# Three adaLN vectors summed on GpSimd beside the attention, a fourth on VectorE in the first FFN, and P scaled on VectorE

## The chip, the cores and the metric

One core of one Trainium2 chip runs the kernel; nothing is shared with other cores. The time is that of one execution on the device, in microseconds (us); lower is better. A profile is taken of one execution of its own.

## The reference, cut to what matters

Two layers of a diffusion transformer over 512 latent tokens of 1024 channels, with 256 context tokens. The first layer mixes tokens by attention (4 heads of global attention, 4 of windowed attention), the second by a Fourier transform; each layer ends in a gated FFN with a width-3 convolution. Six vectors for each layer (shift, scale and gate of both sub-layers) come from a matrix-vector product with the conditioning vector; four of the first layer's six are what the change is about.

```python
def adaln_params(cond, w, bias):
    m = jax.nn.silu(cond) @ w + bias                     # (1024) @ (1024, 6 * 1024)
    return jnp.split(m[..., None, :], N_MOD, axis=-1)
...
def attend(q, k, v, sink=None):
    s = jnp.einsum('bqkgd,bskd->bkgqs', q, k, preferred_element_type=F32) * (HEAD_DIM ** -0.5)
    ...
        p = jax.nn.softmax(s, axis=-1)
    return jnp.einsum('bkgqs,bskd->bqkgd', p.astype(v.dtype), v)
...
    for i in range(DEPTH):
        sh1, sc1, g1, sh2, sc2, g2 = adaln_params(c, mod_w[i], mod_b[i])
        h = modulate(rms_norm(x, norm_g[i, 0]), sh1, sc1)
        ...
        x = x + g1 * rms_norm(y, norm_g[i, 1])
        h = modulate(rms_norm(x, norm_g[i, 2]), sh2, sc2)
        x = x + g2 * rms_norm(conv_ffn(h, ...), norm_g[i, 3])
```

## The kernel before

All of it is fp32. A product is made of three (`mm3`, L90 to L92): both operands are split into a high part (a ScalarE copy to fp32r) and a low part (the difference, on VectorE or now and then GpSimd; `split`, L113). Activations lie with channels on partitions: `xT`, `yT`, `hh` and `hl` are 128 x 8 x 512.

The stages, in order: the start (shift and scale, keys and values of two heads, up to about 100 us); the other projections; the attention with the rest of the query projections beside its first heads (about 120 to 275 us); the output projection and the first FFN; the Fourier mixer; the second FFN.

*The attention.* Eight heads, one after the other, each with four blocks of 128 queries (32 blocks). For a block TensorE makes the scores (`S`), VectorE their maximum (L854) and the exponent's bias (L857 in heads 0 to 3, L862 in heads 4 to 7), ScalarE the exponential into `P` with its sum (L864). In heads 4 to 7, which have a sink, L867 and L868 add the sink's term to the sum. L869 takes the reciprocal, and L870 multiplies the 128 x 768 (or 640, or 512) block of P by it, on GpSimd. TensorE transposes P (`PT`, L786), ScalarE and VectorE split it, and TensorE multiplies it with the values (`O`). The products with the values run one head behind the scores.

*Work beside the attention.* `rest` is a Python generator that issues the query projections of heads 2 to 7 (`gm`, with their rotary part in `roped`, L637 to L643, partly on GpSimd); `gem0` issues the adaLN products. After each half block the kernel advances one of them by the number of steps in its table `FILL`: `rest` in heads 0 to 3, `gem0` in heads 4 to 7.

*The adaLN vectors.* A matrix-vector product of 1024 x 1024 for each. Vectors 0 and 1 of layer 0 are made in the start. `gemv_pe` makes 2 to 5: for two vectors at a time it loads eight 1 MB tiles, 128 rows of the matrix each, and TensorE multiplies each with one column of the conditioning vector, in four column groups (L405); then a copy (L409), four transposes (L412), and one addition of the bias. `gemv_jobs` makes the six of layer 1 in the first FFN: eight multiply-adds of 128 x 1024 on VectorE (L376, L379), the sum over partitions by TensorE (L384), two transposes. There, `pump(gem, ...)` advances it by one step for each of 19 hidden tiles (11 in the first half, 8 in the second) and by two for each of 8 output tiles, 35 steps in all; a vector takes five steps.

*What sets the order.* The kernel is traced in the order of the Python code, and a planner with a model of each engine's times orders the instructions on each engine; an engine then executes its list in order and waits where a semaphore isn't yet there. Work traced late may be put early if its inputs are there. Loads go through SyncE's queue, in order. All weights pass through three 1 MB buffers (`raw`, L121).

*Who needs the vectors.* Vector 2 (as `der[:, 0, 1]`) is the gate after the output projection, 3 and 4 make the input of the first FFN, right after it. Vector 5 (as `der[:, 0, 3]`) is the gate after the first FFN, some 400 us later.

Of the kernel before, what the change touches and what calls it, by code (L numbers as in the profile page):

```python
# [34 lines left out]
# what is traced where: how far work of one kind runs ahead of another kind's  # L35
# [6 lines left out]
# products that keep the PE's clock up: at the start, before the first sums' use, before the second FFN  # L42
# [25 lines left out]
def kernel(ctx: ExitStack, tc: tile.TileContext, a):  # L68
# [25 lines left out]
    # issued after another one on the same engine  # L94
# [4 lines left out]
    # work that must not be issued ahead of the last instruction traced before a fence on its engine  # L99
# [61 lines left out]
    # products that keep the PE's clock up where it would have to wait  # L161
# [4 lines left out]
    # sums over channels: four column tiles of the PE hold a quarter of the tokens each  # L166
# [5 lines left out]
    # 1 / sqrt(sum / D + eps)  # L172
# [10 lines left out]
    # the same where only the time until the end counts: sums on all partitions at once  # L183
# [14 lines left out]
    # one quarter of the tokens per quadrant of partitions: side by side, then to all partitions  # L198
# [12 lines left out]
    # h = x * am * R + bm for several channel tiles, shared out over the engines  # L211
# [15 lines left out]
    # squares of y: summed over channel tiles by GpSimd, the last one by the PE  # L227
    class YStat:
# [8 lines left out]
        def add(self, pps, src, hs):  # L237
# [9 lines left out]
            # the halves of the last one share a tile where they come one after the other  # L247
# [26 lines left out]
    # x += gate * rms_norm(y) for one channel tile  # L274
# [11 lines left out]
    # x += gate * rms_norm(y); then the next sub-layer's modulated input  # L286
# [56 lines left out]
        # the factors: tokens on partitions, or on all partitions  # L343
# [23 lines left out]
    # adaLN off the critical path: products and sums on DVE, the sum over partitions on the PE  # L367
    def gemv_jobs(jobs, pps):
        for l, v in jobs:
            acc = mk(cp, [P, D], F32, "gacc", 1)  # L370
            for kk in range(4):
                w = raw([P, 2, D], a["mod_r"][v, kk])
# [9 lines left out]
            ps = mk(pps, [P, T], F32, "misc", 2)  # L382
            for j in range(4):
                PE.matmul(ps[32 * j:32 * j + 32, :256], lhsT=ones32, rhs=acc[:, j * 256:(j + 1) * 256], start=True,  # L384
                          stop=True)
            rs = mk(cp, [P, T], F32, "sq", 2)
            S.copy(out=rs[:, :256], in_=ps[:, :256])
            tp = mk(pps, [P, T], F32, "misc", 2)
            for b in range(2):
                PE.transpose(out=tp[:, b * P:(b + 1) * P], in_=rs[:, b * P:(b + 1) * P], identity=ident)  # L390
# [4 lines left out]
            derive(l, v)  # L395
# [1040 lines left out]
```

## Time and profile before

| | |
|---|---|
| median of 3 runs | 1181.5 us (1178.45 to 1182.66) |
| span of the profiled execution, first to last instruction | 1176.5 us |
| the profiled execution's own time | given as its span alone |
| instructions | 17,135 |
| mean granted TensorE clock | 0.988 of full speed |
| TensorE (PE) busy | 1134.0 us, 96% |
| VectorE (DVE) busy | 751.6 us, 64% |
| ScalarE (ACT) busy | 512.2 us, 44% |
| GpSimd (POOL) busy | 201.1 us, 17% |
| moved by DMA | 145.18 MB |

A row of a group reads: line, engine, operation, tile written <- tiles read, shapes, number of instructions | busy us in all, mean ns of one | idle time of the engine just before them, and what ended it. A row of the timeline reads: start, duration (both us), engine, line, operation, tiles, shapes; "x2" joins two instructions that follow each other, with the time from the first's start to the last's end. A row of a stretch has the busy time of each engine in it, then the granted clock, the DMA engines' busy share and GB/s. TensorE's busy time is modelled; a matmul's record overlaps with the next one's, so path shares tell more of it than sums of durations. The busy time of an instruction on VectorE or GpSimd includes what it waits after it has been issued.

### The profile page before, as it was taken

How to read it: one execution, taken by the hardware profiler on the slowest of the kernel's cores; microseconds unless marked ns; L12 is line 12 of the kernel's file. 1: busy time of each engine (PE TensorE's matmuls, PEld its weight loads, DVE VectorE, ACT ScalarE, POOL GpSimd, SP SyncE). 2: the span in 40 equal slices, each digit the busy share in tenths (PEclk: the TensorE clock that was granted, in tenths of full speed). 3: DMA queues.
4: the chain of work that ended last, by engine and by line, in shares of the span. 5: the costliest groups of instructions: out<-in, count | busy, mean ns of one | idle time of the engine just before them, and what ended most of it. 6: DMA issues, size and time to landing. Idle time of an engine off the chain costs nothing.

```text
span 1176.5 us, 17135 instructions
## 1 busy us (share of the span) xinstructions
PE 1134.0 (96%) x6878; PEld 946.1 (80%) x6878; DVE 751.6 (64%) x1215; ACT 512.2 (44%) x887; POOL 201.1 (17%) x213
## 2 busy tenths in 40 slices
PE   7999999999999999999999998988999999999995
PEld 4689898679898877777878998877788888888895
DVE  4673777675779685756665568988966532255555
ACT  3332356566554434322444445646644332234342
POOL 1132534222320000000000153663000000000013
PEclk9999999999999999999999999998999999999998
DMA  9432110874115353666622301621233222332112
GB/s 371 187 127 72 37 36 7 298 306 152 65 43 209 108 208 110 237 238 225 233 90 56 116 11 35 210 81 60 72 108 103 73 84 99 108 108 72 54 55 72
DMA packets 27127, 145.18 MB, mean 123 GB/s; under 512 B 2724, under 2 KB 7460, under 8 KB 14120
## 3 DMA queue, kind: packets, MB, share of 16 engines
q1 hardware_dynamic: 27048, 144.09, 35.0%
q8 instruction: 54, 0.88, 0.3%
q14 instruction: 25, 0.20, 0.1%
HBM read 141.98 MB, written 2.10 MB: 122 GB/s over the span
## 4 chain that ended last, share of the span: by engine, by line
PE 84%; DVE 11%; DMA 1%; ACT 1%; issue 1%; POOL 1%; SPq 0%; DVEq 0%; ACTq 0%; POOLq 0%
PE mm L90 24%; PE mm L92 23%; PE mm L91 23%; DVE md_t L278 2%; PE PT L786 2%; PE gm L405 1%; DVE hl L333 1%; PE O L90 1%; DVE wl L113 1%; DVE xT L280 1%; PE S L90 1%; PE O L91 1%; PE O L92 1%; PE S L92 1%; DMA xT<-in_xT 1%
## 5 line engine op out<-in xcount | busy, mean ns | idle before, releaser
L113 DVE TENSOR_TENSOR wl<-raw,wh 128x1024 fp32r<-128x1024 f32 (+1 forms) x139 | 167.6, 1210 | 207.8 <-ACT wh L113 207.5
L90 PE MATMUL mm<-hh,wh 128*128 128x512 f32 (+2 forms) x728 | 276.1, 379 | 0.0
L92 PE MATMUL mm<-hh,wl 128*128 128x512 f32 (+2 forms) x728 | 275.7, 379 | 0.0
L91 PE MATMUL mm<-hl,wh 128*128 128x512 f32 (+2 forms) x728 | 275.4, 378 | 0.0
L113 ACT CAST wh<-raw 128x1024 fp32r<-128x1024 f32 (+2 forms) x151 | 149.6, 999 | 183.4 <-PE mm L91 141.9
L90 PEld LDWEIGHTS mm<-hh,wh 128*128 128x128 f32 x728 | 137.7, 189 | 29.3 <-issue 1.2
L92 PEld LDWEIGHTS mm<-hh,wl 128*128 128x128 f32 x728 | 137.7, 189 | 27.9
L91 PEld LDWEIGHTS mm<-hl,wh 128*128 128x128 f32 x728 | 137.8, 189 | 27.5
L253 POOL TENSOR_TENSOR gacc<-gacc,sq 128x256 f32<-128x256 f32 (+1 forms) x35 | 31.5, 900 | 681.3 <-ACT sq L251 680.5
L90 PE MATMUL mm<-xh,wh 128*128 128x512 f32 (+1 forms) x368 | 131.5, 357 | 0.0
L91 PE MATMUL mm<-xl,wh 128*128 128x512 f32 (+1 forms) x368 | 130.6, 355 | 0.0
L92 PE MATMUL mm<-xh,wl 128*128 128x512 f32 (+1 forms) x368 | 130.5, 355 | 0.0
L90 PEld LDWEIGHTS mm<-xh,wh 128*128 128x128 f32 x368 | 69.2, 188 | 12.4 <-issue 1.2
L91 PEld LDWEIGHTS mm<-xl,wh 128*128 128x128 f32 x368 | 69.1, 188 | 11.1
L92 PEld LDWEIGHTS mm<-xh,wl 128*128 128x128 f32 x368 | 69.0, 187 | 11.0
L113 ACT CAST xh<-cv 128x512 fp32r<-128x512 f32 x44 | 27.3, 620 | 100.9 <-DVE cv L1008 100.9
L995 DVE SCALAR_TENSOR_TENSOR cv<-mm,cols,cv 128x511 f32<-128x511 f32 x83 | 61.8, 745 | 11.4 <-ACT cv L994 11.4
L994 ACT ACTIVATE cv<-mm,cols 128x512 f32<-128x512 f32 x83 | 64.2, 774 | 10.4 <-PE mm L92 10.4
L997 DVE SCALAR_TENSOR_TENSOR cv<-mm,cols,cv 128x511 f32<-128x511 f32 x83 | 62.2, 749 | 2.2
L1007 ACT ACTIVATE cv<-cv 128x512 f32<-128x512 f32 x44 | 27.8, 631 | 71.2 <-DVE cv L997 68.7
L379 DVE SCALAR_TENSOR_TENSOR gacc<-raw,scol,gacc 128x1024 f32<-128x1024 f32 x42 | 53.8, 1281 | 4.5 <-DMA raw<-in_mod_r 4.1
L91 PE MATMUL mm<-hl,xh 128*128 128x256 f32 (+1 forms) x160 | 47.3, 296 | 3.6 <-DVE hl L333 2.8
(358 smaller groups left out, 2238.7 us busy)
## 6 DMA issues: line engine op xcount, KB each, us to landing
raw<-in_w_up SPq DMA_DIRECT2D x44, 1024.0 KB, 5.0
raw<-in_mod_r SPq DMA_DIRECT2D x24, 1024.0 KB, 5.0
raw<-in_mod_p SPq DMA_DIRECT2D x16, 1024.0 KB, 6.4
raw<-in_w_down SPq DMA_DIRECT2D x16, 896.0 KB, 4.6
raw<-in_w_down SPq DMA_DIRECT2D x16, 512.0 KB, 3.7
raw<-in_w_in SPq DMA_DIRECT2D x6, 1024.0 KB, 5.0
raw<-in_w_out SPq DMA_DIRECT2D x4, 1024.0 KB, 6.0
raw<-in_w_f SPq DMA_DIRECT2D x8, 512.0 KB, 4.4
```

Source lines behind the costliest of these rows:

```text
L90: i = PE.matmul(out, lhsT=ah, rhs=bh, start=start, stop=False)
L91: PE.matmul(out, lhsT=ah, rhs=bl, start=False, stop=False)
L92: return i, PE.matmul(out, lhsT=al, rhs=bh, start=False, stop=stop)
L113: i = S.copy(out=h, in_=src), eng.tensor_tensor(out=l, in0=src, in1=f(h), op=ALU.subtract)
L253: G.tensor_tensor(out=self.acc[:, sl], in0=self.acc[:, sl], in1=sq[:, sl], op=ALU.add)
L278: m = V.scalar_tensor_tensor(out=t, in0=yT[:, k, hs], scalar=der[:, l, gi, k:k + 1], in1=R, op0=ALU.mult, op1=ALU.mult)
L379: held(V.scalar_tensor_tensor(out=acc, in0=w[:, i, :], scalar=scol[:, 0, k:k + 1], in1=acc, op0=ALU.mult, op1=ALU.add))
L786: PE.transpose(out=pt[:, j * P:(j + 1) * P], in_=Ps[j][:, off:off + P], identity=ident)
L994: S.activation(out=cv, in_=ps, func=AF.Identity, bias=bc, scale=wc[1])
L995: V.scalar_tensor_tensor(out=cv[:, 1:], in0=ps[:, :T - 1], scalar=wc[0], in1=cv[:, 1:], op0=ALU.mult, op1=ALU.add)
L997: V.scalar_tensor_tensor(out=cv[:, :T - 1], in0=ps[:, 1:], scalar=wc[2], in1=cv[:, :T - 1], op0=ALU.mult, op1=ALU.add)
L1007: S.activation(out=cg, in_=cg, func=AF.Silu)
```

## The change

Four things are edited; everything else in the diff is comments that are taken out.

- `gemv_pe` goes. `gemv_pool` makes the vectors 2, 3 and 4 in halves of 512 columns: GpSimd multiplies each 128 x 512 piece of the matrix by the conditioning vector's column (in place in `raw`) and adds it to `pacc`, eight pieces for each half; four small products on TensorE sum over the partitions and bring the result to partitions at once; VectorE adds the bias. A step of the generator has two pieces.
- It is advanced by one step after each of the 32 query blocks, in all heads. Heads 4 to 7 have no entries in `FILL` any more. A vector takes nine steps, three take 27.
- Vector 5 becomes the first job of `gemv_jobs` in the first FFN, ahead of layer 1's six: seven jobs of five steps.
- L870 is issued on VectorE instead of GpSimd.

The matrix is laid out anew in memory: twelve tiles of 1 MB for `gemv_pool`, and four more for `gemv_jobs`, in place of sixteen for `gemv_pe`.

```diff
 FILL = [[1, 0, 1, 2, 3, 2, 1, 2],
...
-        [2, 1, 1, 0, 0, 1, 1, 2],
-        [2, 0, 0, 1, 1, 0, 2, 0],
-        [1, 0, 1, 0, 1, 0, 1, 0],
-        [2, 0, 1, 0, 0, 0, 1, 1],
-        [1, 0, 0, 0, 2, 1, 2, 0]]
+        [2, 1, 1, 0, 0, 1, 1, 2]]
...
     def gemv_jobs(jobs, pps):
...
-                w = raw([P, 2, D], a["mod_r"][v, kk])
+                w = raw([P, 2, D], a["mod_r"][6 * l + v - 5, kk])
...
-    def gemv_pe(pps):
-        for j in range(2):
-            ps = mk(pps, [P, T], F32, "gm", 1)
-            for k in range(KC):
-                w = raw([P, 2048], a["mod_p"][j, k])
-                for q in range(4):
-                    PE.matmul(ps[32 * q:32 * q + 32, :], lhsT=spad[:, k, :], rhs=w[:, q * T:(q + 1) * T],
-                              start=k == 0, stop=k == KC - 1)
-                yield
...
+    def gemv_pool(vs, pool, pps):
+        for v in vs:
+            for h in range(2):
+                acc = mk(pool, [P, T], F32, "pacc", 1)
+                for k in range(KC):
+                    if k % 4 == 0:
+                        w = raw([P, 4, T], a["mod_a"][v - 2, h, k // 4])
+                    sc = scol[:, 0, k:k + 1]
+                    t = w[:, k % 4, :] if k else acc
+                    G.tensor_scalar(out=t, in0=w[:, k % 4, :], scalar1=sc, scalar2=0.0, op0=ALU.mult, op1=ALU.add)
+                    if k:
+                        G.tensor_tensor(out=acc, in0=acc, in1=t, op=ALU.add)
+                    if k % 2:
+                        yield
+                ps = mk(pps, [P, T], F32, "PT", 2)
+                for b in range(4):
+                    PE.matmul(ps[:, 2 * b:2 * b + 2], lhsT=acc[:, b * P:(b + 1) * P], rhs=ones32[:, :2], start=True,
+                              stop=True)
+                mo = C_MB + v * KC + 4 * h
+                V.tensor_tensor(out=mods[:, 0, v, 4 * h:4 * h + 4],
+                                in0=ps[:, :8].rearrange("p (b r) -> p b r", r=2)[:, :, 0], in1=cols[:, mo:mo + 4],
+                                op=ALU.add)
+            derive(0, v)
             yield
...
-            gem0 = gemv_pe(aps)
+            gem0 = gemv_pool([2, 3, 4], at, aps)
...
-                    G.tensor_scalar(out=pr[:, :n], in0=pr[:, :n], scalar1=mx[:, 4:5], scalar2=0.0,
-                                    op0=ALU.mult, op1=ALU.add)
+                    V.tensor_scalar(out=pr[:, :n], in0=pr[:, :n], scalar1=mx[:, 4:5], scalar2=None, op0=ALU.mult)
...
                     for i in range(2):
                         pump(pend)
-                        pump(rest if is_a else gem0, FILL[head][2 * j + i])
+                        if is_a:
+                            pump(rest, FILL[head][2 * j + i])
+                    pump(gem0)
...
-                 gemv_jobs([(1, v) for v in range(6)], pps))
+                 gemv_jobs([(0, 5)] + [(1, v) for v in range(6)], pps))
...
-    mod_p = i['mod_w'][0].reshape(KC, P, 3, 2048)[:, :, 1:].transpose(2, 0, 1, 3)
+    mod_a = mw[0, :, :, 2:5].reshape(2, 4, P, 3, 2, T).transpose(3, 4, 0, 2, 1, 5)
```

More of the change, by code (lines that the diff above doesn't have):

```diff
@@ L365, in derive, with gemv_end @@
             V.tensor_tensor(out=der[:, l, n, :], in0=mods[:, l, v, :], in1=ng(l, n), op=ALU.mult)
+    def gemv_end(l, v, acc, pps, tag, bufs):
+        ps = mk(pps, [P, T], F32, tag, bufs)
+        for j in range(4):
+            PE.matmul(ps[32 * j:32 * j + 32, :256], lhsT=ones32, rhs=acc[:, j * 256:(j + 1) * 256], start=True,
+                      stop=True)
+        rs = mk(cp, [P, T], F32, "sq", 2)
+        S.copy(out=rs[:, :256], in_=ps[:, :256])
+        tp = mk(pps, [P, T], F32, tag, bufs)
+        for b in range(2):
+            PE.transpose(out=tp[:, b * P:(b + 1) * P], in_=rs[:, b * P:(b + 1) * P], identity=ident)
+        mo = C_MB + l * 48 + v * KC
+        V.tensor_tensor(out=mods[:, l, v, :].rearrange("p (j b) -> p j b", b=2),
+                        in0=tp[:, :256].rearrange("p (b j r) -> p j b r", b=2, r=32)[:, :, :, 0],
+                        in1=cols[:, mo:mo + KC].rearrange("p (j b) -> p j b", b=2), op=ALU.add)
+        derive(l, v)
     def gemv_jobs(jobs, pps):
@@ L381, in gemv_jobs @@
                 yield
[L382 to L390, printed above, removed]
@@ L1414, in _layout @@
     xT = chan(i["x"][0]).reshape(P, KC, 2, HT).transpose(0, 2, 1, 3)
[L1415 removed]
+    out.update(cols=cols, gqk=np.concatenate(rep[1:], 1), xT=xT, cT=chan(i["ctx"][0]), mod_s=mod_s, mod_r=mr[5:], mod_a=mod_a, w_kva=kva, w_in=np.stack(wi),
                w_out=w_out, w_up=w_up, w_f=w_f, w_ny=wf[:, P])
```

20 lines of the change are left out of this document (2 added, 18 removed).

## The prediction

> **What bounds the kernel now.** I read the summary first, then the chain of work that ended last, then the busy times of the stretches in which the change lies.
>
> ```profile
> span 1176.5 us, 17135 instructions
> PE 1134.0 (96%) x6878; PEld 946.1 (80%) x6878; DVE 751.6 (64%) x1215; ACT 512.2 (44%) x887; POOL 201.1 (17%) x213
> PE 84%; DVE 11%; DMA 1%; ACT 1%; issue 1%; POOL 1%; SPq 0%; DVEq 0%; ACTq 0%; POOLq 0%
> ...
> core 0: us, PE busy (x) PEld busy (x) DVE busy (x) ACT busy (x) POOL busy (x), PEclk, DMA share, GB/s
> 120.00:201.00 81.00, 77.70 (x550) 72.67 (x549) 61.01 (x124) 41.94 (x74) 32.17 (x31) 1.00 0.08 27
> 201.00:260.00 59.00, 59.00 (x426) 39.52 (x425) 42.01 (x102) 34.67 (x83) 13.25 (x17) 1.00 0.74 272
> 420.00:600.00 180.00, 180.00 (x799) 141.97 (x798) 117.99 (x131) 62.11 (x82) 0.00 (x0) 1.00 0.57 204
> ```
>
> TensorE carries 84% of the chain and GpSimd stands idle for 83% of the span, so the idea of moving sums from the one to the other looks sound at first sight. The two stretches of the attention differ. In the first, 120 to 201 us (heads 0 to 3), VectorE is busy for 61.0 of 81 us and GpSimd for 32.2. In the second, 201 to 260 us (heads 4 to 7), TensorE never pauses: the adaLN products that the change removes are mixed into it. The chain of that stretch shows how much they are.
>
> ```profile
> by line: PE gm L405 27.7%; PE PT L786 14.7%; PE O L90 11.2%; PE O L92 7.8%; PE O L91 7.7%; PE S L90 4.6%; PE S L846 4.0%; PE S L847 4.0%; PE S L848 3.9%; PE S L92 3.6%; PE S L91 3.2%; PE S L851 2.7%; PE PT L816 2.3%; PE gm L412 1.5%; PE S L
> ```
>
> **What TensorE loses and gets.** L405, the adaLN products, is 27.7% of 59 us = 16.3 us of the path, and L412, the transposes behind it, 1.5% = 0.9 us. Both go: -17.2 us, all of it in heads 4 to 7. Back come six groups of four products of a 128x128 block with two columns, one group for each half vector. The kernel has a line of that form in its Fourier part, and the first FFN has the form of the seventh job:
>
> ```profile
> 702.75 0.95 PE L349 MATMUL misc<-ones,yT 128*128 128x2 f32 x8
> 413.20 0.64 PE L384 MATMUL misc<-gacc,ones 128*32 128x256 f32 x8
> ```
>
> Four such products (eight records) take 0.95 us, so six groups take 5.7 us, half of it in heads 0 to 3. TensorE alone would gain 17.2 - 5.7 = 11.5 us. The seventh job adds 0.64 us and two transposes to the first FFN, where TensorE is full: +1 us. Its eight VectorE instructions are hidden there: VectorE is busy for 118 of 180 us between 420 and 600, and eight more at the durations of the rows below (one of 0.75, seven of 1.28 us) are 9.7 us; without that cover they would cost all of it.
>
> **What the P scaling costs VectorE.** L870 leaves GpSimd. The nearest VectorE row is L376, the same operation with a per-partition factor from SBUF to SBUF.
>
> ```profile
> L870 POOL TENSOR_SCALAR P<-P,mx 128x768 f32<-128x768 f32 x16 | 14.7, 916 | 39.1 <-DVE mx L869 31.8 <-PE PT L786 5.7 <-DVE qrs L150 1.5
> L870 POOL TENSOR_SCALAR P<-P,mx 128x640 f32<-128x640 f32 x8 | 7.3, 907 | 27.5 <-ACT th L113 7.0 <-DVE mx L869 6.4 <-DVE mx L862 5.3
> L870 POOL TENSOR_SCALAR P<-P,mx 128x512 f32<-128x512 f32 x8 | 5.6, 697 | 18.1 <-DVE mx L869 9.9 <-PE PT L786 3.7 <-ACT hh L113 2.8
> L376 DVE TENSOR_SCALAR gacc<-raw,scol 128x1024 f32<-128x1024 f32 x4 | 3.0, 752 | 17.0 <-PE misc L384 17.0
> L379 DVE SCALAR_TENSOR_TENSOR gacc<-raw,scol,gacc 128x1024 f32<-128x1024 f32 x34 | 43.6, 1281 | 2.6 <-DMA raw<-in_mod_r 2.2
> ```
>
> 752 ns for 1024 elements is 0.73 ns each: 16 x 0.56 = 9.0 us in heads 0 to 3, and 8 x 0.47 + 8 x 0.38 = 6.8 us in heads 4 to 7. The Trainium skill (VectorE: DVE Perf Modes, "Mode 2x_2P") lets such an operation take two fp32 elements a cycle at 0.96 GHz; by that, an estimate, the 21,504 elements a partition would need 11.2 us and not 15.8, and the whole sum would be 4.6 us lower. I go by the row.
>
> **What GpSimd gets.** Each half vector is 8 multiplications and 7 additions of 128x512. The multiplication is the third L870 row, 0.70 us; the addition is L643 where nothing disturbs it, 1.29 us (first row below). 8 x 0.70 + 7 x 1.29 = 14.6 us, six halves 87.7 us, in 27 steps of which one is traced with each of the 32 query blocks: 3.25 us a step. GpSimd keeps 32.2 - 14.7 = 17.5 us of other work in heads 0 to 3 (the rotary part of the queries). With 16 steps (52 us) it has 69.5 us of work there, where it had 32.2.
>
> **The price is in how GpSimd and VectorE meet.** The timeline shows pairs of rows, GpSimd first, VectorE next:
>
> ```profile
> 125.89 1.29 POOL L643 TENSOR_TENSOR yT<-yT,sq 128x512 f32<-128x512 f32 x1
> 126.08 1.12 DVE L148 TENSOR_TENSOR qtm<-qrs 128x8 f32<-128x8 f32 x1
> 127.64 0.17 DVE L148 TENSOR_TENSOR qtm<-qrs 128x8 f32<-128x8 f32 x1
> ...
> 142.79 1.28 POOL L643 TENSOR_TENSOR yT<-yT,sq 128x512 f32<-128x512 f32 x1
> 142.83 1.27 DVE L153 TENSOR_SCALAR qtm<-qst 128x8 int32<-128x8 int32 x1
> ...
> 197.52 2.54 POOL L113 TENSOR_TENSOR hl<-yT,hh 128x512 fp32r<-128x512 f32 x2
> 198.23 0.59 DVE L857 SCALAR_TENSOR_TENSOR mx<-mx,qsc 128x1 f32<-128x1 f32 x1
> ...
> 170.34 1.22 DVE L113 TENSOR_TENSOR wl<-raw,wh 128x1024 fp32r<-128x1024 f32 x1
> 170.51 2.19 POOL L643 TENSOR_TENSOR yT<-yT,sq 128x512 f32<-128x512 f32 x1 [0.25 <-DVE yT L641]
> ...
> 130.69 1.43 POOL L637 TENSOR_TENSOR sq<-sq,gacc 128x256 f32<-128x256 f32 x2 [3.51 <-DVE qst L632]
> 130.72 0.68 DVE L113 TENSOR_TENSOR ql<-PT,qh 128x512 fp32r<-128x512 f32 x1
> ```
>
> An instruction on eight elements that takes 0.17 us alone takes 1.12 us when it meets a GpSimd addition, and ends just when that one ends (127.20 against 127.18). A VectorE multiplication by a scalar waits in the same way (142.83), and so does the one-element L857 (198.23: 0.59 us and not 0.16). At 170.51 it is the other way round: GpSimd's 1.29 us become 2.19 us, since VectorE was first. An instruction with one operand in PSUM (130.72) isn't touched. The Trainium skill (SBUF — State Buffer, "Who interferes with whom") calls this an exclusive lock on a shared port pair in which the later one "fully blocks"; these rows agree, and the page names no size from which on it holds.
>
> So I charge each VectorE instruction that has two SBUF operands, or one and a scalar, what is left of the GpSimd instruction it meets: (0.70² + 1.29²) / (2 x (0.70 + 1.29)) = 0.54 us, times the share of time in which GpSimd is busy. The bounds are 0 (it never meets one) and 0.54 (GpSimd never pauses). Heads 0 to 3 have 16 scalings and 16 L857, and by my count some 20 others (low parts of weights and values, rotary products, steps of the inverse root) that meet GpSimd now only at times. If that stretch becomes 91 us, GpSimd is busy for 69.5 / 91 = 0.76 of it, and a wait is 0.41 us. VectorE then needs 61.0 + 9.0 + 32 x 0.41 + 20 x 0.41 = 91.3 us, against the 81 us that the stretch takes now: +10 us. By the bounds it is 0 (VectorE's 70 us lie beside TensorE's 81) and +18 (98.1 us).
>
> Heads 4 to 7 need 59 - 17.2 + 2.9 = 44.7 us of TensorE. VectorE needs 42.0 + 6.8 = 48.8 us without waits (ScalarE, at 34.7 of 59 us, loses two copies, which changes nothing). Three instructions of each block (scaling, L862, L868) are of the kinds that wait, 48 in all. GpSimd has eleven steps left, 35.8 us, or 21 us if the planner starts the first half vector in the idle time ahead of the attention:
>
> ```profile
> 117.55 1.75 POOL L637 TENSOR_TENSOR sq<-sq,gacc 128x256 f32<-128x256 f32 x2 [20.97 <-DVE qst L632]
> ```
>
> At 21 to 36 of 60 us a wait is 0.19 to 0.32 us, and VectorE needs 48.8 + 9 to 15 = 58 to 64 us. I take 61, +2 us; the bounds are -10.2 (no wait) and +16 (all at 0.54).
>
> **Queues.** The loads stay sixteen of 1 MB: twelve in the attention, four in the first FFN. In the attention their place in the three raw tiles now comes ahead of the last two query weights, and SyncE's queue is in order, so those weights may be issued later than now.
>
> ```profile
> 79.59 15.15 SPq L122 DMA_DIRECT2D raw<-in_w_in  x2
> raw<-in_w_in SPq DMA_DIRECT2D x6, 1024.0 KB, 5.0
> 138.35 1.22 DVE L113 TENSOR_TENSOR wl<-raw,wh 128x1024 fp32r<-128x1024 f32 x1
> ```
>
> They are issued by 95 us, take 5.0 us to land and are split from 138 us on: 38 us of cover, so I take nothing, and 5 us for each of the two if the cover goes. Behind a late GpSimd sum stand the rotary additions of the next queries on GpSimd, and on TensorE, whose queue is in order too, everything behind the small product that reads the sum; I take nothing for that in the sum and make it a rival.
>
> **The sum.** +10 (heads 0 to 3) +2 (heads 4 to 7) +1 (first FFN) = +13 us on a span of 1176.5 us. No time of the profiled execution is shown but its span; the median of the runs is 5.0 us above it. 1181.5 + 13 = 1194.5, say 1194 us.
>
> **Rivals.** *TensorE's relief comes through (faster).* VectorE has 20 us of idle time in the first stretch, and the chain after 150 us lies on TensorE; if GpSimd does much of its work before 120 us and VectorE's waits stay below some 11 us in heads 0 to 3 and 10 us in heads 4 to 7, they are covered. Then heads 4 to 7 fall to VectorE's 48.8 us (-10.2), heads 0 to 3 take up to 2.9 us more, the FFN 1: -6 to -9 us, and TensorE's own 11.5 - 1 us at most: 1171 to 1175, I say 1173. For it speaks the 27.7%; against it that VectorE, at 61 of 81 us, has hardly room for 9 us more and 52 meetings. *A wash.* Waits of half the size that I charge: +5 and -4 and +1, 1183 us. *TensorE is held by GpSimd's sums.* If the plan puts the six small products too early, TensorE stands for about one step (3.25 us) and the lock's delays in it (some 1 us) at each: -11.5 + 1 + 6 x 4.2 = +15, 1197 us. Against it: six places only, with slack if the plan leaves some. *The change doesn't do what it says*: excluded, since L405 and L870 are gone by the diff.
>
> **How the numbers follow.** Contention decides (my forecast, 1194): 0.40. Relief comes through (1173): 0.32. Wash (1183): 0.16. TensorE held (1197): 0.12. About 0.5%, 5.9 us, is what a measurement of this kernel can tell from no change. Slower by more than that: most of the first and the fourth, 0.50. Faster: 0.32. Within: 0.18. The range takes in the relief with its bounds and the contention nearly to its upper ones (+10 to +18 and +2 to +16, not both at the end): 1168 to 1211. The forecast's own range is 1187 to 1211.
>
> **What would show it.** L405 and L412 gone and heads 4 to 7 with idle time on TensorE. VectorE's L857 with a mean well above 0.16 us and the scaling above 0.56 us would show the waits, GpSimd's multiplications above 0.70 us the other side. The first stretch, up to the last of head 3's scalings, longer by about 10 us and VectorE in it above 90% busy. If L857 stays at 0.16 us, or if the second stretch shrinks by 10 us and the first holds, the relief has won. Waits of TensorE for GpSimd's `pacc` of over 10 us in all show the fourth case. I am wrong altogether if the planner spreads GpSimd's work where VectorE reads PSUM.

## The result, and the profile after

The changed kernel takes 1194.91 us (median; 1191.34 to 1197.17) beside 1181.51 us of the kernel before (1178.45 to 1182.66): ratio 1.0114, 95% interval 1.0088 to 1.0141. It is 13 us slower; the profiled spans, 1189.6 and 1176.5 us, differ by as much. Lines have moved: the functions' names are the same, L854 is now L856, L857 L859, L862 L864, L868 L870, L870 L872, L643 L645, L786 L788, L816 L818, and the splits stand in L109. GpSimd's multiplications are L408, its additions L410, the small products L415.

The summary and the chain of work that ended last, of the changed kernel:

```profile
span 1189.6 us, 17015 instructions
PE 1132.8 (95%) x6800; PEld 952.5 (80%) x6800; DVE 791.0 (66%) x1260; ACT 511.7 (43%) x886; POOL 267.4 (22%) x271
PE 77%; DVE 14%; POOL 3%; issue 2%; ACT 2%; DMA 2%; DVEq 0%; SPq 0%; ACTq 0%; POOLq 0%
```

The same stretches as before the change, and the chain of heads 4 to 7 by line:

```profile
core 0: us, PE busy (x) PEld busy (x) DVE busy (x) ACT busy (x) POOL busy (x), PEclk, DMA share, GB/s
120.00:201.00 81.00, 72.60 (x490) 66.12 (x489) 70.03 (x129) 34.96 (x60) 57.07 (x55) 0.96 0.26 92
201.00:260.00 59.00, 48.65 (x310) 40.72 (x309) 48.52 (x95) 30.48 (x68) 43.86 (x39) 0.94 0.33 110
420.00:600.00 180.00, 180.00 (x800) 142.02 (x799) 119.79 (x134) 60.28 (x80) 0.00 (x0) 1.00 0.57 205
```

```profile
by line: POOL pacc L410 30.1%; POOL raw L408 9.0%; DMA raw<-in_w_out 8.8%; issue 7.0%; POOL hl L109 6.4%; DVE tl L109 3.6%; DVE P L872 3.5%; PE PT L415 3.1%; PE gm L86 2.7%; POOL pacc L408 2.4%; POOL yT L645 2.1%; PE O L86 2.0%; PE gm L87 1
```

TensorE pauses for 8.4 of 81 us and for 10.4 of 59 us, where it had 3.3 and none, and its granted clock is 0.96 and 0.94 there. L405 and L412 are gone from the chain of heads 4 to 7, and the small products (L415) have 3.1% of it. GpSimd's sums stand in their place (L410 alone has 30.1%), and behind them a load of the output weights. The first FFN (third row) is as it was.

The instructions that can meet, grouped by shape (the first five over the whole run, L864 over 201 to 275 us, L870 over 96 to 275 us; the last row is of the kernel before):

```profile
L410 POOL TENSOR_TENSOR pacc<-pacc,raw 128x512 f32<-128x512 f32 x42 | 57.3, 1364 | 2.9
L408 POOL TENSOR_SCALAR raw<-raw,scol 128x512 f32<-128x512 f32 x42 | 35.7, 864 | 8.0 <-DMA raw<-in_mod_a 8.0
L408 POOL TENSOR_SCALAR pacc<-raw,scol 128x512 f32<-128x512 f32 x6 | 4.2, 696 | 20.5 <-PE PT L415 20.5
L872 DVE TENSOR_SCALAR P<-P,mx 128x768 f32<-128x768 f32 x16 | 14.9, 933 | 0.3
L859 DVE SCALAR_TENSOR_TENSOR mx<-mx,qsc 128x1 f32<-128x1 f32 x16 | 6.0, 373 | 0.2
L864 DVE TENSOR_SCALAR mx<-mx,nsink 128x1 f32<-128x1 f32 x16 | 3.2, 203 | 0.0
L870 DVE TENSOR_TENSOR mx<-mx 128x1 f32<-128x1 f32 x15 | 6.6, 441 | 0.3 <-ACT mx L869 0.3
...
L857 DVE SCALAR_TENSOR_TENSOR mx<-mx,qsc 128x1 f32<-128x1 f32 x16 | 2.9, 183 | 0.3
```

The one-element L859 has 373 ns where it had 183, GpSimd's multiplications 864 where 696 is what they take undisturbed: both sides wait. L864, also one element, does not: it had 211 ns before and has 203 now.

*Where the 13 us are.* Four stages, cut at moments that every kernel has. The start is the first ScalarE copy of a query weight near 107 us; it moves by up to 4 us between executions with the first loads, so it is subtracted. "A" runs from there to the maximum of block 0, "B" to that of block 16 (head 4), "C" to that of block 31, "D" to the end of the span. Each figure is how much longer the stage is than in the kernel before, in us, from the timelines of one execution each; the last column is the timed result, (ratio - 1) x 1181. The names e1 to e16 stand for the experiments below. One execution says little about 1 to 2 us: e13 changes nothing ahead of block 0 and has +1.5 in A, and e2 has +2.6 in D while its timed result is no change. B repeats better: 0.0 to -0.2 in e2, e3 and e13, and +6.5 to +6.9 in the changed kernel, e5, e15 and e16.

| kernel | A | B | C | D | sum | timed |
|---|---|---|---|---|---|---|
| changed kernel | +6.0 | +6.6 | +3.1 | -1.0 | +14.7 | +13.4 |
| e1, scaling on GpSimd | +6.6 | +15.2 | +14.1 | -2.6 | +33.3 | +33.8 |
| e2, before + scaling on VectorE | 0.0 | -0.2 | 0.0 | +2.6 | +2.4 | -0.4 |
| e3, before without the products | 0.0 | -0.1 | -10.5 | -0.6 | -11.2 | -13.1 |
| e4, 12 of 90 sums | 0.0 | +2.6 | -9.3 | -3.1 | -9.8 | -9.2 |
| e5, weights held | +6.0 | +6.6 | -7.0 | +5.1 | +10.7 | +9.2 |
| e6, scaling on ScalarE | +6.7 | +3.7 | -0.4 | -0.5 | +9.5 | +10.4 |
| e10, other forms | +5.9 | +6.4 | +3.5 | -1.6 | +14.2 | +14.4 |
| e11, all three | +6.1 | +3.3 | -6.3 | +8.5 | +11.5 | +9.9 |
| e13, fifth vector alone | +1.5 | 0.0 | -2.0 | +0.1 | -0.4 | -1.9 |
| e14, half | +3.6 | +9.8 | -2.0 | +3.7 | +15.1 | +15.0 |
| e15, first half left out | +4.1 | +6.5 | +3.6 | -1.1 | +13.2 | +13.1 |
| e16, last half left out | +6.7 | +6.9 | -0.2 | 0.0 | +13.3 | +11.1 |

Almost half of the changed kernel's loss lies in A, before the first block. The timeline of the changed kernel there, GpSimd first, then VectorE:

```profile
123.97 2.40 POOL L408 TENSOR_SCALAR raw<-raw,scol 128x512 f32<-128x512 f32 x2
126.34 1.40 POOL L639 TENSOR_TENSOR sq<-sq,gacc 128x256 f32<-128x256 f32 x2
127.82 1.27 POOL L645 TENSOR_TENSOR yT<-yT,sq 128x512 f32<-128x512 f32 x1
129.08 2.70 POOL L408 TENSOR_SCALAR raw<-raw,scol 128x512 f32<-128x512 f32 x4
```

```profile
128.00 1.12 DVE L145 SCALAR_TENSOR_TENSOR qtm<-qtm,qst 128x8 f32<-128x8 f32 x1
129.15 0.63 DVE L146 SCALAR_TENSOR_TENSOR qrs<-qtm,qrs 128x8 f32<-128x8 f32 x1
129.81 0.64 DVE L144 TENSOR_TENSOR qtm<-qrs 128x8 f32<-128x8 f32 x1
130.48 0.64 DVE L145 SCALAR_TENSOR_TENSOR qtm<-qtm,qst 128x8 f32<-128x8 f32 x1
131.15 0.64 DVE L146 SCALAR_TENSOR_TENSOR qrs<-qtm,qrs 128x8 f32<-128x8 f32 x1
```

These are steps of head 0's inverse root, a chain of nine small instructions of which each needs the last: 125.76 to 131.79 us, 6.0 us where it took 2.7 (126.08 to 128.81). In 129.08 to 131.78 four multiplications stand on GpSimd and four steps on VectorE, one after the other. GpSimd's rotary addition, behind two multiplications, ends at 129.09 and not at 127.18, and TensorE, which transposes its result, waits (the waits of 118 to 140 us, then two stretches):

```profile
PE PT L818 <- POOL yT L645: 4.0, 1, 4.0
```

```profile
124.00:130.00 6.00, 2.01 (x14) 1.77 (x14) 5.73 (x11) 0.73 (x2) 5.92 (x7) 0.92 0.53 175
130.00:136.00 6.00, 4.87 (x22) 4.14 (x21) 4.28 (x8) 0.46 (x1) 4.36 (x6) 0.51 0.01 3
```

TensorE stands for 4 of the first 6 us, and then has half its clock: another 4.87 x 0.49 = 2.4 us of its work lost.

The chain of 118 to 140 us tells what of this sets the start of block 0. It runs over the root, the VectorE operation behind it that releases TensorE's next products (L629), and these products at half the clock (132.65 to 136.0 us). The root gives 3.3 us of the 6.0, two instructions ahead of it (L707 with 1.26 us for 0.71, L150 with 0.47 for 0.17) some 0.9, and the clock, by an estimate, half of those 3.4 us. TensorE's wait for the rotary addition isn't on this chain; it is the pause ahead of the slow clock.

In C, heads 4 to 7, block 22 starts 4.6 us better than block 16 did: TensorE's relief arrives. Then comes the load of the output weights, whose first copy the plan now puts beside head 5 (rows of three timelines of the changed kernel, then two of the kernel before):

```profile
235.44 0.33 SPq L118 DMA_DIRECT2D raw<-in_w_out  x1
240.65 1.04 ACT L109 CAST wh<-raw 128x1024 fp32r<-128x1024 f32 x1 [7.15 <-DMA raw<-in_w_out]
242.12 0.69 PE L86 MATMUL O<-th,wh 128*128 128x384 f32 x1 [6.09 <-ACT th L109]
...
247.35 0.33 SPq L122 DMA_DIRECT2D raw<-in_w_out  x1
252.43 2.00 ACT L113 CAST wh<-raw 128x1024 fp32r<-128x1024 f32 x2
```

SyncE issues it when GpSimd's last addition ahead of it has ended (235.43 us) and a `raw` tile is free; ScalarE's next copy waits for it 7.15 us, and TensorE behind ScalarE 6.09. The kernel before issues the same load 12 us later, and no engine waits for it. So the load isn't late by itself. It is late for the place that the plan gave its copy in ScalarE's list. From block 22 to block 24 the kernel loses 11.8 us and gets 4.1 back by block 31.

### The profile page after: what moved, and what is told of

It is laid out like the page before. It is cut to its first block, busy times and chain, and to the rows that moved or that the text cites. A ratio compares the mean times of both kernels' runs of the same rounds, so it can differ in the third digit from the quotient of the medians.

```text
span 1189.6 us, 17015 instructions
## 1 busy us (share of the span) xinstructions
PE 1132.8 (95%) x6800; PEld 952.5 (80%) x6800; DVE 791.0 (66%) x1260; ACT 511.7 (43%) x886; POOL 267.4 (22%) x271
## 4 chain that ended last, share of the span: by engine, by line
PE 77%; DVE 14%; POOL 3%; issue 2%; ACT 2%; DMA 2%; DVEq 0%; SPq 0%; ACTq 0%; POOLq 0%
PE mm L86 23%; PE mm L88 23%; PE mm L87 23%; DVE md_t L274 2%; POOL pacc L410 1%; DVE wl L109 1%; DVE hl L329 1%; DVE P L872 1%; DVE xT L276 1%; DVE mx L856 1%; PE misc L535 1%; DVE md_t L217 1%; DMA raw<-in_w_up 1%; DVE tl L109 1%; PE misc L200 1%
## 5 line engine op out<-in xcount | busy, mean ns | idle before, releaser
L109 DVE TENSOR_TENSOR wl<-raw,wh 128x1024 fp32r<-128x1024 f32 (+1 forms) x139 | 168.5, 1216 | 202.3 <-ACT wh L109 201.9
L109 ACT CAST wh<-raw 128x1024 fp32r<-128x1024 f32 (+2 forms) x151 | 149.7, 1000 | 189.7 <-PE mm L87 146.3
L86 PEld LDWEIGHTS mm<-xh,wh 128*128 128x128 f32 x368 | 69.3, 188 | 12.6 <-issue 1.6
L998 DVE SCALAR_TENSOR_TENSOR cv<-mm,cols,cv 128x511 f32<-128x511 f32 x83 | 61.8, 745 | 11.5 <-ACT cv L997 11.4
L109 ACT CAST xh<-cv 128x512 fp32r<-128x512 f32 x44 | 27.3, 621 | 96.9 <-DVE cv L1011 96.9
L392 DVE SCALAR_TENSOR_TENSOR gacc<-raw,scol,gacc 128x1024 f32<-128x1024 f32 x49 | 62.8, 1281 | 4.5 <-DMA raw<-in_mod_r 4.0
L410 POOL TENSOR_TENSOR pacc<-pacc,raw 128x512 f32<-128x512 f32 x42 | 57.3, 1364 | 2.9
```

The costliest lines, as they stand in the source:

```text
L86: i = PE.matmul(out, lhsT=ah, rhs=bh, start=start, stop=False)
L109: i = S.copy(out=h, in_=src), eng.tensor_tensor(out=l, in0=src, in1=f(h), op=ALU.subtract)
L392: held(V.scalar_tensor_tensor(out=acc, in0=w[:, i, :], scalar=scol[:, 0, k:k + 1], in1=acc, op0=ALU.mult, op1=ALU.add))
L410: G.tensor_tensor(out=acc, in0=acc, in1=t, op=ALU.add)
L998: V.scalar_tensor_tensor(out=cv[:, 1:], in0=ps[:, :T - 1], scalar=wc[0], in1=cv[:, 1:], op0=ALU.mult, op1=ALU.add)
```

## The experiments

Theories at this point: (1) GpSimd's sums and VectorE's instructions shut each other out, and that makes the loss; (2) GpSimd is simply late, and what stands behind it in its queue or waits for its tiles comes late; (3) the scaling itself is too much for VectorE.

**e1: the scaling back on GpSimd.**

```diff
-                    V.tensor_scalar(out=pr[:, :n], in0=pr[:, :n], scalar1=mx[:, 4:5], scalar2=None, op0=ALU.mult)
+                    G.tensor_scalar(out=pr[:, :n], in0=pr[:, :n], scalar1=mx[:, 4:5], scalar2=0.0,
+                                    op0=ALU.mult, op1=ALU.add)
```

> The changed kernel with P's scaling back on GpSimd, so that the adaLN sums alone are moved. Theory "VectorE and GpSimd shut each other out" (the waits make the loss): GpSimd gets 14.7 + 12.9 us more to do and has then 69.5 + 14.7 = 84 us of work in heads 0 to 3, and a scaling that stands behind a sum on GpSimd waits for it; no gain, 1192 to 1210 us, L859 of VectorE above 0.35 us as now. Rival "the scaling itself is too much for VectorE": its 9.0 + 6.8 us come off, 1180 to 1186 us.

Measured: 1212.11 us, ratio 1.0286 (1.0260 to 1.0313), slower still. This is just above the range expected, and theory 3 fails here. The waits of 120 to 275 us say how:

```profile
PE PT L788 <- POOL P L872: 24.8, 9, 5.0
```

TensorE stands 25 us for P behind sums in GpSimd's queue. With the sums on GpSimd the scaling can't stay there: of the two edits of the attention the second is what keeps the first from costing 34 us.

**e2: the scaling on VectorE alone** (the same edit of L870 in the kernel before).

> The kernel before with P's scaling on VectorE and nothing else changed. Shutting out: GpSimd keeps only 17.5 us of work in heads 0 to 3 and nearly none in heads 4 to 7, so the scaling takes 0.55 to 0.7 us and its 70 and 49 us on VectorE lie beside TensorE's 81 and 59: 1178 to 1184 us. Rival "the scaling itself is too much for VectorE": +9 us or more, 1188 to 1195 us.

Measured: 1179.31 us, ratio 0.9997 (0.9983 to 1.0010). No cost: VectorE is busy for 67.5 of 81 us and 47.4 of 59 us, beside TensorE. The scaling's 128 x 768 rows take 689 ns on the mean here and 933 in the changed kernel.

**e3: the products left out.** `gemv_pe` gives the biases in the four vectors' place, without loads and products.

> The kernel before with the products of the four adaLN vectors (second to fifth) left out with their loads, the bias alone stands in their place: the most that taking them off TensorE can bring. If TensorE's share of the path is what the chain says: 17.2 us of products and transposes gone, heads 4 to 7 at VectorE's 42 us, 1163 to 1168 us. Rival "another limit takes over at once" (VectorE's chain of one block, the loads of the output weights): 4 to 8 us of it come, 1174 to 1178 us.

Measured: 1165.89 us, ratio 0.9889 (0.9865 to 0.9913), -13 us (-10 to -16 by the interval) of the 17.2 that the chain showed. That is the most that can come from moving the products.

**e4: twelve of the 90 sums.**

```diff
-                    G.tensor_scalar(out=t, in0=w[:, k % 4, :], scalar1=sc, scalar2=0.0, op0=ALU.mult, op1=ALU.add)
-                    if k:
-                        G.tensor_tensor(out=acc, in0=acc, in1=t, op=ALU.add)
+                    if k % 4 == 0:
+                        G.tensor_scalar(out=acc, in0=w[:, 0, :], scalar1=sc, scalar2=0.0, op0=ALU.mult, op1=ALU.add)
```

> The changed kernel with 12 of GpSimd's 90 instructions of the sums left in (78 are left out, so three adaLN vectors are not computed in full); loads, small products on TensorE and the scaling on VectorE stay. If GpSimd's sums make the loss, by shutting VectorE out or by coming late: heads 0 to 3 return to 81 to 84 us, heads 4 to 7 fall to 49 to 52 us, 1171 to 1177 us, with L859 at 0.16 to 0.2 us and the scaling at 0.55 to 0.65 us. If the scaling on VectorE makes it: 1188 us or more, and L859 stays above 0.3 us.

Measured: 1170.71 us, ratio 0.9922 (0.9898 to 0.9946). So the change with most of GpSimd's sums left out is a gain of 9 us, and those sums cost some 23 us (+13.4 against -9.2). Rows of e4, by shape, and its first load of the output weights:

```profile
L871 DVE TENSOR_SCALAR P<-P,mx 128x768 f32<-128x768 f32 x16 | 11.0, 689 | 0.3
L858 DVE SCALAR_TENSOR_TENSOR mx<-mx,qsc 128x1 f32<-128x1 f32 x16 | 2.5, 153 | 0.2
```

```profile
212.11 16.60 SPq L118 DMA_DIRECT2D raw<-in_w_out  x4
```

A is 0.0, B +2.6 (about what the prediction put the small products at, 2.9; no run takes them alone), C -9.3. The load goes out 23 us earlier than in the changed kernel. e4 can't tell theory 1 from 2, since it takes away both.

**e5: the output weights held back**, so that they may not be split ahead of head 7's third block.

```diff
                     if head == 7 and j == 2:
+                        fence()
                         ow = out_weights(0, None)
+                        fences.clear()
```

> The changed kernel with one point in its order: the split of the first output weights (whose load stands behind GpSimd's last sums for a raw tile) may not be put ahead of head 7's third block on any engine. Theory "late weights hold ScalarE's queue": ScalarE's 7.2 us of waiting for that load and TensorE's 6.1 us behind it at 235 to 248 us go, and 5 to 10 us with them, 1185 to 1190 us. Rival "they only fill time that the waits between VectorE and GpSimd cost anyway": 1193 to 1196 us.

Measured: 1188.69 us, ratio 1.0078 (1.0055 to 1.0101), some 4 us better than the changed kernel, though the two intervals overlap, and less than the 5 to 10 us expected. The starts of the blocks show what the hold does. Up to block 22 they agree with the changed kernel's within 0.1 us; from block 22 to block 24 the changed kernel loses 11.8 us and e5 2.1. So the stall is real. C becomes 10.1 us shorter (+3.1 to -7.0), but D gives 6.1 back (rows of two timelines of e5):

```profile
251.01 0.33 SPq L118 DMA_DIRECT2D raw<-in_w_out  x1
265.84 1.98 ACT L109 CAST wh<-raw 128x1024 fp32r<-128x1024 f32 x2
```

The first three of the four loads go out at 236.74, 245.47 and 251.01 us and land some 5 us later, while ScalarE copies none of them before 265.84 us, and the output projection's first products come behind that. What D loses is the price of the hold, which waits too long; by then the weights have been there for some 10 us.

**e6: the scaling on ScalarE.**

```diff
-                    V.tensor_scalar(out=pr[:, :n], in0=pr[:, :n], scalar1=mx[:, 4:5], scalar2=None, op0=ALU.mult)
+                    S.activation(out=pr[:, :n], in_=pr[:, :n], func=AF.Copy, scale=mx[:, 4:5])
```

> The changed kernel with P's scaling on ScalarE. GpSimd's sums stay as they are. Shutting out: VectorE loses its 27 us of scalings with the 11 us of waits in them, ScalarE has room for some 32 x 0.6 us (it is busy for 35 of 81 and 30 of 59 us), 1182 to 1189 us. Rival "GpSimd's sums come late, in order, ahead of the rotary additions and the loads": they are no shorter than before, 1192 to 1197 us.

Measured: 1189.46 us, ratio 1.0088 (1.0068 to 1.0108), just above the range of theory 1 and below that of the rival. Its interval overlaps with the changed kernel's, so the timed result doesn't tell the two apart; stage B does. It falls from +6.6 to +3.7, near the 2.6 of e4 with few sums: inside the blocks of heads 0 to 3 the scaling on VectorE beside the sums costs about 3 us. A stays at +6.7.

**e10: one-element operations in another form.**

```diff
-                        V.scalar_tensor_tensor(out=mx[:, 1:2], in0=mx[:, 0:1], scalar=-1.0, in1=sc,
-                                               op0=ALU.mult, op1=ALU.mult)
+                        V.tensor_scalar(out=mx[:, 1:2], in0=mx[:, 0:1], scalar1=-1.0, scalar2=sc,
+                                        op0=ALU.mult, op1=ALU.mult)
...
-                        V.tensor_tensor(out=mx[:, 2:3], in0=mx[:, 2:3], in1=mx[:, 3:4], op=ALU.add)
+                        V.tensor_scalar(out=mx[:, 2:3], in0=mx[:, 2:3], scalar1=1.0, scalar2=mx[:, 3:4],
+                                        op0=ALU.mult, op1=ALU.add)
```

> The changed kernel with two one-element operations of each block written as tensor_scalar (one element times a constant, then by or plus a second one read as the scalar), the form of L864, which took 0.20 us throughout although GpSimd's sums ran beside it. Nothing of GpSimd's work changes. Shutting out hangs on the form: L859 falls from 0.37 to 0.16 to 0.2 us and L870 from 0.44 likewise, 7 us less on VectorE, in the chain of each block; the scaling still waits; 1186 to 1192 us. Rival "any two-operand instruction waits, whatever its form": both stay above 0.35 us, 1193 to 1197 us. Rival "lateness of GpSimd makes the loss": they fall and the time stays, 1193 to 1197 us.

The rows by shape, 96 to 275 us:

```profile
L859 DVE TENSOR_SCALAR mx<-mx,qsc 128x1 f32<-128x1 f32 x16 | 3.3, 208 | 0.2
L870 DVE TENSOR_SCALAR mx<-mx 128x1 f32<-128x1 f32 x15 | 3.1, 206 | 1.3 <-ACT mx L869 1.1
```

The waits hang on the form: 373 to 208 and 441 to 206 ns, with the same work on GpSimd. And the time stays: 1194.08 us, ratio 1.0122 (1.0101 to 1.0143). So these waits cost nothing that can be measured, though the expectation of theory 1 had them on the path. The Trainium skill (SBUF — State Buffer, "Who interferes with whom") has a VectorE instruction with two SBUF inputs contend with a GpSimd instruction that reads SBUF, and one with at most one such input, outside the two-port modes, not. The trace agrees, if an operand that is read as the scalar doesn't count as an input: 206 to 208 ns beside the same sums.

**e11: the three together** (e5, e6 and e10).

> The changed kernel with the two one-element forms, P's scaling on ScalarE and the output weights held back, together: nothing of a block's chain on VectorE meets GpSimd's sums any more but the inverse root and the low parts. If the waits between VectorE and GpSimd and the late weights make the 24 us that the sums cost: 1172 to 1180 us. If GpSimd's work is simply late: 1185 us or more, with TensorE waiting for the rotary additions.

Measured: 1188.96 us, ratio 1.0084 (1.0065 to 1.0103); the expectation of theory 1 failed, and the gains don't add. A is still +6.1; the inverse root's nine steps keep their form with two tensors. B is at +3.3, near e4's 2.6. Beside the changed kernel C gains 9.4 us and D loses 9.5. With the attention done sooner TensorE runs out of work (two stretches of e11, then rows of two of its timelines):

```profile
255.00:270.00 15.00, 12.52 (x66) 9.97 (x65) 10.23 (x27) 11.70 (x26) 0.00 (x0) 0.84 0.00 1
270.00:285.00 15.00, 15.00 (x81) 12.53 (x80) 6.14 (x10) 6.44 (x11) 0.00 (x0) 0.96 0.21 72
...
247.19 0.33 SPq L118 DMA_DIRECT2D raw<-in_w_out  x1
265.63 1.98 ACT L109 CAST wh<-raw 128x1024 fp32r<-128x1024 f32 x2
```

Three loads of the output weights are issued by 247.19 us (the first at 233.68), and in 255 to 270 us nothing moves by DMA; ScalarE copies the weights from 265.63 us on. TensorE waits there for ScalarE, 1.77 us for a scaled P (265.79) and 0.50 for copied weights (266.72), while the projection's products, its other work, are held back. As in e5 it is the hold that is paid for here, and not a late load. So e11 shows that A isn't touched by the forms and the scaling's place, and that what the sums add in B nearly goes. What it says of C and D is blurred by its own edit. The next four runs were to take A and the output weights apart, and to try a version between the two kernels.

**e15: the first half vector's sums left out.**

```diff
+                    out_ = v == 2 and h == 0
+                    if not out_:
                         ...
+                    elif k % 4 == 0:
+                        G.tensor_scalar(out=acc, in0=w[:, 0, :], scalar1=sc, scalar2=0.0, op0=ALU.mult, op1=ALU.add)
```

> The changed kernel with the sums of the first half vector left out but for two multiplications (13 GpSimd instructions, those that it starts at 96 us, ahead of head 0). Theory "the start of head 0 is held": in the changed kernel the nine small steps of head 0's inverse root take 0.62 to 1.12 us and not 0.17, the rotary addition comes 2 us late, TensorE stands and its clock falls to 0.51 in 130 to 136 us, and block 0 starts 4.4 us late; this goes, 5 to 7 us, 1187 to 1190 us. Rival "the waits inside the blocks make the loss" or "the late output weights set the end": 1192 to 1196 us.

Measured: 1191.77 us, ratio 1.0111 (1.0085 to 1.0137), no gain. It doesn't speak against the theory, for the edit missed its target: the planner put the second half's multiplications, which work in place and need no accumulator, where the first half's had been (GpSimd's timeline of e15):

```profile
122.36 4.79 POOL L410 TENSOR_SCALAR raw<-raw,scol 128x512 f32<-128x512 f32 x5
127.12 1.40 POOL L643 TENSOR_TENSOR sq<-sq,gacc 128x256 f32<-128x256 f32 x2
```

The rotary step waits behind them until 127.12 us and A is still +4.1; TensorE's clock is 0.50 in 130 to 136 us. The plan fills a place with whatever work is ready early.

**e16: the last half vector's sums left out** (the same edit with `v == 4 and h == 1`).

> The changed kernel with the sums of the last half vector left out but for two multiplications (13 GpSimd instructions). Theory "GpSimd's late sums hold the raw tiles, and the output weights stand behind them": the first of those loads is issued some 10 us earlier than 235 us, ScalarE's 7.2 us of waiting for it go, 1184 to 1189 us. Rival "the loss is made before, in the blocks": 1192 to 1196 us.

Measured: 1189.75 us, ratio 1.0094 (1.0067 to 1.0121), which isn't told from the changed kernel's 1.0114. This one missed as well: the half's two loads are still in SyncE's queue ahead of the output weights, whose first load went out at 237.99 us, and ScalarE still waits 5.8 us for it. Inconclusive.

**e13: the fifth vector alone.** The kernel before with `gemv_jobs([(0, 5)] + ...)`, as in the change, and `gemv_pe` for the vectors 2 to 4.

> The kernel before with one part of the change alone: the fifth vector is summed on VectorE in the first FFN, vectors two to four stay on TensorE, GpSimd and the scaling stay as they were. A quarter of L405 and of L412 goes, 4.3 us, and the seventh job gives 1 us back: 1177 to 1179 us. Rival "VectorE's seventh job comes on the path of the first FFN": 1181 us or more.

Measured: 1177.77 us, ratio 0.9984 (0.9967 to 1.0002): -1.9 us, which the interval doesn't quite tell from none. It is the only part of the move that may pay. The 4.3 us of C came to 2.0, and A lost 1.5 with no sums on GpSimd at all: TensorE's clock was 0.73 in 132 to 138 us, after the same short pauses (1.4 of 6 us) that leave it at 1.00 in the kernel before (two stretches before, then the same of e13):

```profile
126.00:132.00 6.00, 4.58 (x33) 3.80 (x32) 5.06 (x15) 1.19 (x2) 2.49 (x3) 1.00 0.02 4
132.00:138.00 6.00, 6.00 (x45) 5.92 (x44) 3.09 (x7) 4.29 (x6) 2.98 (x4) 1.00 0.00 0
...
126.00:132.00 6.00, 4.59 (x34) 3.80 (x33) 5.62 (x16) 1.18 (x2) 3.14 (x3) 0.99 0.00 0
132.00:138.00 6.00, 6.00 (x35) 6.00 (x35) 3.12 (x6) 0.77 (x1) 2.71 (x3) 0.73 0.02 4
```

**e14: half.** The vectors 2 and 3 on TensorE, 4 on GpSimd, advanced in heads 1 to 3, its first multiplication not ahead of head 1; 5 and the scaling on VectorE. Heads 4 to 7 have entries in `FILL` again, for `gemv_pe`.

```diff
-            gem0 = gemv_pool([2, 3, 4], at, aps)
+            gem0 = gemv_pe(aps)
+            gem4 = gemv_pool([4], at, aps)
...
+                if head == 1:
+                    fence()
...
+                    if 1 <= head < 4:
+                        pump(gem4)
```

> A version between the two: vectors two and three on TensorE as before (half of L405), the fourth alone on GpSimd, not started before head 1, the fifth on VectorE in the first FFN, P's scaling on VectorE. TensorE loses 8.6 us and gets 1.9 + 1 us. If the loss comes from the start of head 0 and from sums that end late, neither happens with 29 us of sums in heads 1 to 3: 1175 to 1178 us. If it comes from the waits in the blocks: a third of them stays, some 4 us, and 1180 to 1182 us.

Measured: 1193.12 us, ratio 1.0127 (1.0094 to 1.0160). That is outside both ranges expected. With a third of the sums it loses as much as the changed kernel, most of it (B, +9.8) at one place. Between block 3 and block 6 it falls back by 7 us (VectorE's and TensorE's timelines, while GpSimd adds without a pause from 149.14 to 159.41 us):

```profile
151.24 1.22 DVE L148 TENSOR_TENSOR qtm<-qrs 128x8 f32<-128x8 f32 x1
152.38 0.15 DVE L903 RECIPROCAL mx<-mx 128x1 f32<-128x1 f32 x1
152.49 0.17 DVE L149 SCALAR_TENSOR_TENSOR qtm<-qtm,qst 128x8 f32<-128x8 f32 x1
152.57 1.63 DVE L904 TENSOR_SCALAR P<-P,mx 128x768 f32<-128x768 f32 x1
154.12 1.23 DVE L150 SCALAR_TENSOR_TENSOR qrs<-qtm,qrs 128x8 f32<-128x8 f32 x1
```

```profile
154.26 1.29 PE L818 MATMUL PT<-con,P 128*128 128x128 f32 x5 [3.46 <-DVE P L904]
```

The additions met the second inverse root, with the scaling in the same queue. The changed kernel has its own second root at 149 to 156 us, and there GpSimd stands for 7.19 us until 156.01, waiting for TensorE; its steps take 0.15 to 0.17 us. So what GpSimd's sums stand beside counts for more here than how many they are; no run moves only their place. (A flaw of this version: the fence held one multiplication only; the other seven, in place, still ran from 99 us on, and A is +3.6.)

## Why the prediction was right, and where its working was not

The sum came to +13 us, and the timed difference is +13.4. That they agree so closely is in part luck. By the stages it is +12.6 where +10 was reckoned (A and B), +3.1 where +2 was (C) and -1.0 where +1 was (D), and the causes inside the first two are not those that were summed. Its mechanism, GpSimd's sums shutting VectorE's instructions out so that the relief is lost, is there in the rows, but it is only part of the loss.

*TensorE's relief of 11.5 less 1 us.* Right in size: e3, without any of the products, gains 13 us where the chain had 17.2, and e4, with the small products and the seventh job in, 9 (6 to 12 by the interval).

*The scaling costs nothing by itself, its meetings do.* Right: e2 is no change, and 689 ns become 933 in the changed kernel. The 0.56 us by which I costed it is somewhat low: a row of 128 x 768 that meets nothing takes 0.61 to 0.62 us (at 200.72 and 155.32 us of the changed kernel), and all 32 take 19.3 us in e2 where the sum had 15.8.

*Heads 0 to 3, +10 us by VectorE's waits in the blocks.* The end of the stage came nearly as predicted (block 16 starts 11.0 us late in the span, 12.6 us with the start subtracted); the cause is split otherwise. I let 52 waits of 0.41 us add up on a VectorE that would be over 90% busy; it is busy for 70.0 of 81 us. What the trace has in their place is a chain of nine steps that each need the last, at the inverse root of head 0 (A, +6.0, with the rotary addition behind multiplications in GpSimd's queue and half the clock after it). No run takes that chain alone away. In the blocks it is +6.6: 2.6 of it are there with few sums (e4), about 3 go with the scaling (e6), and the waits of the 16 one-element L859 are worth nothing that can be measured (e10). The step that failed is the equation of a sum of waits with a loss of time.

*Three instructions of each block in heads 4 to 7 wait.* Two do: the scaling and the addition of the sink's term (now L870). The exponent's bias (now L864), which I charged, stays at 203 ns; the form decides, as e10 shows. The row at 142.83 that I read as a multiplication by a scalar is an integer shift of 128 x 8, so it was no example for a one-element instruction with a scalar.

*Heads 4 to 7, +2 us.* Measured +3.1, for another reason. VectorE isn't the bound (48.5 of 59 us): 4.6 us of relief had come by block 22, and the stall at the output weights took it. "Queues: I take nothing" is the step that failed. I looked at the query weights ahead of the sums, the last of which was issued 50 us later than before (144.34 against 95 us) and cost nothing that the waits show, and not at the loads behind the sums. In e4 these go out from 212 us on and nothing waits for them; in the versions with 77 or more of the sums at 234 to 238 (e1, which is late as a whole, at 252). The kernel before has them at 247 without a wait, so it takes both, the late load and a plan that wants it early. e5 shows what the wait costs inside C, and that no more than some 4 us of it came back in the time with that hold.

*TensorE held by GpSimd's sums.* TensorE never waits for `pacc`; it waited for the rotary addition behind the sums, once, 4.0 us. GpSimd waited for TensorE instead, 20.5 us in three places, since its single accumulator is read by products that the plan puts late (the first group at 154.96 us).

*The first FFN, +1 us.* Too small to be seen: D is -1.0, with TensorE full in both.

*Two slips in the sums.* With all 52 waits at 0.54 us VectorE would need 98.1 us, which is +17 on 81 and not +18. With waits of half the size it would need 80.7 us, less than the 81 there are, so the "+5" of the wash doesn't follow from the formula; heads 0 to 3 would give nothing, and that rival would lie below 1181 us.

What stays open: e4 shows that the sums make the loss, and e2 that the scaling by itself doesn't. How the loss divides between shutting out and lateness is read from the traces, for no run had all the sums without the loss in A, or without both the stall at the output weights and the price of the hold. The 19 us between e11 and e4 lie in A (6.1) and in C and D together (+2.1 against -12.4); how much of the latter e11's own hold makes isn't known. No version that computes all the vectors beat both kernels beyond doubt; e13 comes nearest.

## What to carry to other kernels

An idle engine is no free engine: before work is moved to it, look on the timeline for the chain of short dependent instructions on the neighbour that it can shut out, and for what stands behind it in queues and buffers; a sum of waits over a busy share says neither. Give moved work a place as well as an engine, since work that is ready early takes the first gap, and hold every instruction of it, not the first. Test by the place: where work is left out, the next work may move up into its place (e15), and a third of it in another place can cost as much as all (e14). And read a hold by what waits behind it: e5 and e11 moved a stall to a later stage.

## What the runs showed of the hardware that was not expected

- A one-element instruction on VectorE that reads its second operand as a scalar takes 203 to 208 ns beside GpSimd's sums, and the same arithmetic with two tensors 373 to 441 ns on the mean (153 to 158 with few sums, e4); small steps with two tensors (128 x 8) took up to 1.23 us.
- After a pause of 4 us TensorE's granted clock was 0.51 for the next 6 us. After the same three short pauses, 1.4 us in all and none above 0.71, it was 1.00 once (before) and 0.73 once (e13, which has the same products there), so a profile of one execution can differ by 1 to 2 us there for no reason that the edit gives. The Trainium skill (TensorE: Matmul & The Clock Gate, "Part 1: The HAM clock gate (the "warmup" mystery)") gives a half-rate state after an idle window of about 3.4 us, with windows that run freely. The 0.51 agrees with the half rate; the 0.73 of e13 comes behind no pause of that length and doesn't follow from it.
- The start, up to the first query weights, moved by up to 4 us between the kernels' executions (105.25 to 109.27 us), also among those with all the sums and the loads as in the change (105.28 to 109.19). That is as much as half of some effects looked for; subtracting it made the single profiles agree with the timed results within 2.8 us.
